# Loads and uses of turned tiles behind later weight tiles, two ways' outputs turned by TensorE, queries and keys ahead of the gated unit

## The chip, the cores and the metric

The kernel runs on one core of a Trainium2 chip. The metric is the time of one execution on the device in microseconds, as the median of several runs. The engines are TensorE (PE in the rows), VectorE (DVE), ScalarE (ACT), GpSimd (POOL) and SyncE (SP), which here issues all transfers.

## The reference

Two transformer blocks are computed one after the other for 256 tokens of width 1024, in fp32. The first block has two layers; each is a feed-forward, a mixer of three ways, and a feed-forward. The change touches the mixer of these two layers most:

```python
h = rms_norm(x, mix_norm[l])
uv, c_q, c_kv, k_rope, z, xbc, dt_raw, gates = jnp.split(h @ w_in[l], IN_OFFSETS, axis=-1)
y_a = gmlp_mixer(uv, ...)                # gated unit: gelu(u) * (W_s @ rms_norm(gelu(v)) + b)
y_b = mla_mixer(c_q, c_kv, k_rope, ...)  # causal attention, 8 heads, queries and keys from low ranks
y_c = ssd_mixer(z, xbc, dt_raw, ...)     # state-space way: convolution, scan over two chunks, gate z, norm
g = jax.nn.sigmoid(gates).reshape(bsz, s, N_BRANCH, D_MODEL)
merged = (g[:, :, 0] * (y_a @ w_branch[l, 0]) + g[:, :, 1] * (y_b @ w_branch[l, 1])
          + g[:, :, 2] * (y_c @ w_branch[l, 2]))
x = x + merged @ w_out[l]
```

A feed-forward is `(silu(h @ w_gate) * (h @ w_up)) @ w_down`. There are five of them, two in each layer and one in the second block, whose other parts (a mixer and a cross-attention) run the same helpers.

## The kernel before

**Weights.** All weights are read once from HBM, in tiles of 128 x 1024 fp32 (512 KB) or smaller. `wload` (line 158) issues a tile's transfer from SP into the ring `stage` (5 buffers), has ACT cast it to `whi` (line 165) and DVE subtract that from it into `wlo` (line 166); these two rings have 4 buffers each (`NW`). A product is three TensorE instructions (`mac`, lines 288 to 292): high part by high, high by low, low by high. So ACT can cast a weight tile only when TensorE is through with the tile four before it. `lin_tok` makes a product with tokens on the partitions for both token tiles of 128; eight k-blocks of 512 columns are four weight tiles, and a tile of two k-blocks feeds 12 instructions with 512 columns.

**Turning tiles.** What the next product contracts over has to stand on the partitions, so outputs are transposed. There are two ways. `to_T` (line 258) lets TensorE transpose blocks of 128 x 128 into a PSUM tile `tp`, from which ACT casts the high and DVE subtracts the low part (`split_evac`, lines 187 to 189). `flip` (line 267) lets DVE transpose blocks of 32 x 32 (line 273), writes the tile to a DRAM tile `flips` in four transfers (line 277), and reads it back in one, `flipped` (line 279), so that the blocks land in place; `flip_T` puts `split_evac` behind that. The rows of the next weight are stored in the order that this leaves (`ways`). Turned through DRAM are: the hidden tiles of the feed-forwards (hTh and hTl), the compressed queries and keys (cqT, ckvT), the queries and keys (qT, kT), and the outputs of the three ways: of the gated unit (yaT), of attention (ybT) and of the state-space way (ycT).

**The mixer.** `SEQ` lists its steps: x (the channels of the state-space way), u (the gated unit), q (queries, keys, values), z (its gate), S (the scan), A (attention), g0 to g2 (the gates of the three ways) and b0 to b2 (their output products, with yaT, ybT and ycT). The products of x, u, q, z, g and b stream weights. S and A have small products, exponentials and masks; they get a raised priority (`CPRIO`).

**What sets the order.** The code is written in the order of `SEQ`; a scheduler then sets each engine's stream from priorities and dependencies (weights have the highest priority, `WPRIO`). Each engine runs its stream in that order, and so does SP with its transfers. `issue_after` puts an instruction behind another in the order. The last b step in `SEQ` is b1, and the merged tile `mg` is then turned by `to_T` into mh and ml for the product with `m1_out`.

Of the kernel before, what the change touches and what calls it, by code (L numbers as in the profile page):

```python
# [8 lines left out]
F32 = mybir.dt.float32  # L9
# [7 lines left out]
P = 128  # L17
D = 1024
S = 256
# [12 lines left out]
BUFS = dict(  # L32
    sg=2, hb=1, flip=2, flipped=1,
    cg=2, xb=2, gv=2, gu=2, sq=2, q=2, k=2, kv=4, xs=2, xd=2, y=2, yo=2, jk=2, pr=2, pT0=2, pT1=2, ao=2, L=2, cbm=2, rp=2,
    D1=2, Mb=2, pm=2, XT=2, X=3, s5m0=2, s5x0=2, s5t=4, sq2=2, tg=1, o2=1, vn=2)
SEQ = "x u q z S A g0 b0 g2 g1 b2 b1"
NS, NW = 5, 4
COLS = ((0, 512), (512, 512))
LAST = ((0, 512), (512, 256), (768, 256))
# [27 lines left out]
class Net:  # L67
    def __init__(self, ctx, tc, a, outs):
        self.tc, self.nc, self.a, self.outs = tc, tc.nc, a, outs
        mk = lambda n, b=None, **k: ctx.enter_context(tc.tile_pool(name=n, bufs=b, **k))  # L70
        self.big = mk("big")
        self.sma, self.small = None, {}
        self.junk = mk("junk", 1)
        self.ps = mk("ps", space=PSUM)
        self.dram = mk("dram", 2, space=bass.MemoryType.DRAM)
        self.lane = ""
        self.wdma, self.ahead = [], []
        self.sma = Arena(self, 1536, "small")
        self.stage = self.A([NS, 1024], "stage")
        self.whi, self.wlo = [self.A([NW, 1024], n, F32R) for n in ("whi", "wlo")]  # L80
        nc = self.nc
        self.cst = Arena(self, 1024, "cst")
        self.triu = self.load(self.cst, a["c_triu"], [P, P], "triu")
        self.cmask = self.load(self.cst, a["c_cmask"], [P, P], "cmask")
        self.rowm = self.load(self.cst, a["c_rowm"], [P, 4], "rowm")
        self.ones = self.cst.tile([P, P])
        nc.vector.memset(self.ones, 1.0)
        self.mhalf = self.cst.tile([P, 8])
        nc.vector.memset(self.mhalf, -0.5)
        self.euler = self.cst.tile([P, 16])  # L90
        nc.vector.memset(self.euler, math.e)
        self.x = [self.A([D], f"x{t}") for t in range(2)]
# [58 lines left out]
    def _shape(t, shape):  # L151
# [4 lines left out]
        return t.rearrange("p (a b c) -> p a b c", b=shape[1], c=shape[2])  # L156

    def wload(self, src, shape):
        nc = self.nc
        n = int(np.prod(shape))  # L160
        i = len(self.wdma)
        with self.tc.high_priority(WPRIO):
            s, h, l = [ring[:, i % ring.shape[1], :n] for ring in (self.stage, self.whi, self.wlo)]
            self.wdma.append(self.dma(s, src, 4))
            nc.scalar.copy(h, s)  # L165
            self.wsub = nc.vector.tensor_tensor(l, s, h.bitcast(F32), ALU.subtract).ins  # L166
# [99 lines left out]

    def flip(self, src, w, rows=4):

# [4 lines left out]
        nc.vector.transpose(r, src)  # L273
        d = self.dram.tile([P, 512], F32, name="flips", tag="flips")[:32 * rows, :4 * w]
        to = d.rearrange("(j c) (i e) -> i c j e", c=32, e=w)
        for i in range(4):
            nc.sync.dma_start(out=to[i], in_=r[i * 32:i * 32 + 32].rearrange("p (j e) -> p j e", e=w))
        raw = self.A([512], "flipped")[:32 * rows, :4 * w]
        nc.sync.dma_start(out=raw, in_=d)
        return raw.rearrange("p (a k b) -> p a k b", a=4, b=32)  # L280

    def flip_T(self, src, n, hi, lo, t):

        tok = slice(t * P, (t + 1) * P)
        hi, lo = [z[:, :, tok].rearrange("p k (a b) -> p k a b", b=32) for z in (hi, lo)]
        self.split_evac(self.flip(src, n * 32).rearrange("p a k b -> p k a b"), hi, lo)

# [212 lines left out]
    def mixer1(self, l, norm, nxt):  # L500
# [38 lines left out]


        pas = self.lin_tok(xT, a["m1_cq"][l], 384)
        pbs = self.lin_tok(xT, a["m1_ckv"][l], 296)
# [58 lines left out]
        def heads():  # L601
# [3 lines left out]
            for hf in range(2):  # L605
# [4 lines left out]
                for t in range(2):  # L610
                    p, pk = pqs[t], pks[t]
                    with self.tc.high_priority(EPRIO):
# [27 lines left out]
                        for src, dst in ((q3, qT), (kk, kT)):  # L640
                            z = self.flip(src.rearrange("p b h c -> p (b h c)"), P, 3)
                            act.copy(dst[:96, :, toks[t]].rearrange("p h (a b) -> p h a b", b=32),
                                     z.rearrange("p a h b -> p h a b"))
                qkv.append((qT, kT, vv, sc))
# [15 lines left out]
        def ssd():  # L660
# [18 lines left out]
            for t in range(2):  # L679
# [59 lines left out]
                for g in range(2):  # L739
                    c = slice(g * S, (g + 1) * S)  # L740
                    stt(y[:, c], y[:, c], rg[:, g:g + 1], g_ssd[:, c], ALU.mult, ALU.mult)
                self.flip_T(y, 4, ycT[0], ycT[1], t)

        def attention():
            for hf in range(2):
                qT, kT, vv, sc = qkv[hf]
                for t in range(2):
# [30 lines left out]
                    for h in range(4):  # L778
                        for kb in range(t + 1):
                            pe.matmul(p[:, h * 64:(h + 1) * 64], pT[kb][:, h], vv[kb][:, h], start=kb == 0, stop=kb == t)  # L780
                    o = self.A([4, 64], "ao")
                    tt(o, self._shape(p[:, :256], [4, 64]), sm[:, :, None].to_broadcast([P, 4, 64]), ALU.mult)
                    self.flip_T(o.rearrange("p a b -> p (a b)"), 2, ybT[0][:, hf * 2:hf * 2 + 2],
                              ybT[1][:, hf * 2:hf * 2 + 2], t)
# [29 lines left out]
        for step in SEQ.split():  # L814
            i = int(step[1:] or 0)
            if step[0] == "b":
                branch(i, ys[i], not begun)
# [676 lines left out]
def _prep(inp):  # L1494
# [14 lines left out]
    cqw, ckvw, xbc, zz, uv, gg, uq, ukv, br = [], [], [], [], [], [], [], [], []  # L1509
    ways = (512,), (256, 256), (512,)  # L1510
    for l in range(2):
# [100 lines left out]
```

## Time and profile before

| | |
|---|---|
| median of 3 runs (lowest, highest) | 1687.34 us (1686.46, 1688.99) |
| the profiled execution, its span | 1684.87 us, 1683.2 us |
| TensorE busy, DVE, ACT, GpSimd | 98%, 68%, 54%, 5% of the span |
| mean granted clock of TensorE | 0.996 |
| chain that ended last: TensorE's share | 95% |

The durations below come from the profiled execution. TensorE's instructions are pipelined: the record of one is longer than the distance to the next, so the distance of starts tells what one costs. "Idle" is the time an engine stood still ahead of a group, and behind the arrow stands what ended most of it. PEclk is the clock that TensorE was granted, as a share of 2.4 GHz.

### The profile page before, as it was taken

The numbers are of one execution on the slowest core, as the hardware profiler recorded it, in microseconds if no ns is written. First come the engines' busy times: TensorE is split into PE (matmuls) and PEld (weight loads), VectorE is DVE, ScalarE is ACT, GpSimd is POOL, SyncE is SP. The second block draws the span as 40 slices with busy tenths as digits, with TensorE's granted clock in tenths as the row PEclk, the third lists the DMA queues.
The fourth block names the chain that finished last, engine by engine and source line by source line (L and its number), as shares of the span: only waits on it lengthen the run. The fifth ranks groups of instructions, "written<-read, shape, count | busy, mean of one in ns | idle before, by whom it ended". The sixth has DMA issues, their size and how long they took to land.

```text
span 1683.2 us, 24727 instructions
## 1 busy us (share of the span) xinstructions
PE 1653.3 (98%) x9090; PEld 1412.7 (84%) x9090; DVE 1152.4 (68%) x1904; ACT 904.5 (54%) x1361; POOL 80.7 (5%) x73
## 2 busy tenths in 40 slices
PE   8999999998999999999999989999999999999998
PEld 6888898887888888888988877888899888888888
DVE  5665599756666556665897666799689746756664
ACT  5444476663545444444676645545477555654443
POOL 0000013000000000000121000000010100000000
PEclk9999999999999999999999999999999999999999
DMA  7777577753687757776777645767764224347872
GB/s 258 242 239 246 178 225 235 225 179 122 193 252 249 230 176 237 248 242 184 230 232 232 191 147 188 225 211 235 230 196 144 64 63 154 123 151 246 260 234 98
DMA packets 158986, 337.15 MB, mean 200 GB/s; under 512 B 35984, under 2 KB 76432, under 8 KB 158864
## 3 DMA queue, kind: packets, MB, share of 16 engines
q1 hardware_dynamic: 158864, 335.57, 63.6%
q8 instruction: 71, 1.16, 0.3%
q14 instruction: 51, 0.42, 0.1%
HBM read 312.43 MB, written 23.07 MB: 199 GB/s over the span
## 4 chain that ended last, share of the span: by engine, by line
PE 95%; DVE 1%; ACT 1%; DMA 1%; issue 0%; SPq 0%; POOL 0%; POOLq 0%; DVEq 0%; ACTq 0%
PE mm L290 28%; PE mm L291 28%; PE mm L292 28%; PE tp L206 1%; PE mmm L290 1%; PE mmm L292 1%; PE mmm L291 1%; PE ch L758 1%; PE chs L1005 1%; PE ch L780 1%; PE ch L1143 0%; PE ch L721 0%; ACT whi L165 0%; PE tp L773 0%; PE ch L1138 0%
## 5 line engine op out<-in xcount | busy, mean ns | idle before, releaser
L166 DVE TENSOR_TENSOR wlo<-stage,whi 128x1024 fp32r<-128x1024 f32 (+3 forms) x552 | 659.6, 1199 | 331.6 <-ACT whi L165 313.1
L165 ACT CAST whi<-stage 128x1024 fp32r<-128x1024 f32 (+3 forms) x552 | 568.4, 1035 | 445.1 <-PE mm L292 366.0
L291 PE MATMUL mm<-wlo,xh 128*128 128x512 f32 (+3 forms) x1264 | 484.2, 385 | 0.0
L292 PE MATMUL mm<-whi,xl 128*128 128x512 f32 (+4 forms) x1264 | 481.0, 385 | 0.0
L290 PE MATMUL mm<-whi,xh 128*128 128x512 f32 (+3 forms) x1264 | 468.1, 385 | 0.1
L291 PEld LDWEIGHTS mm<-wlo,xh 128*128 128x128 f32 x1264 | 237.8, 188 | 45.7 <-DVE wlo L166 0.2
L290 PEld LDWEIGHTS mm<-whi,xh 128*128 128x128 f32 x1264 | 237.0, 188 | 45.9 <-ACT xh L210 0.5
L292 PEld LDWEIGHTS mm<-whi,xl 128*128 128x128 f32 x1264 | 236.8, 188 | 44.8
L292 PE MATMUL mm<-whi,hTl 128*128 128x512 f32 (+1 forms) x484 | 179.0, 370 | 0.0
L291 PE MATMUL mm<-wlo,hTh 128*128 128x512 f32 (+1 forms) x484 | 179.0, 370 | 0.0
L290 PE MATMUL mm<-whi,hTh 128*128 128x512 f32 (+1 forms) x484 | 178.8, 371 | 0.0
L174 POOL TENSOR_TENSOR small<-small,cst 128x1 f32<-128x1 f32 (+2 forms) x60 | 62.1, 1043 | 1154.1 <-DVE small L172 1110.1
L188 ACT CAST hTh<-flipped 128x512 fp32r<-128x512 f32 (+1 forms) x60 | 35.2, 587 | 132.5 <-DMA flipped<-flips 130.9
L292 PEld LDWEIGHTS mm<-whi,hTl 128*128 128x128 f32 x484 | 91.2, 188 | 15.5
L290 PEld LDWEIGHTS mm<-whi,hTh 128*128 128x128 f32 x484 | 91.2, 189 | 15.3
L291 PEld LDWEIGHTS mm<-wlo,hTh 128*128 128x128 f32 x484 | 91.3, 189 | 15.2
L189 DVE TENSOR_TENSOR hTl<-flipped,hTh 128x512 fp32r<-128x512 f32 (+1 forms) x60 | 38.8, 647 | 79.5 <-ACT hTh L188 75.3
L291 PE MATMUL mm<-xl,whi 128*128 128x256 f32 x320 | 90.7, 284 | 1.1 <-DVE xl L211 1.1
L290 PE MATMUL mm<-xh,whi 128*128 128x256 f32 x320 | 90.3, 284 | 1.2 <-ACT xh L210 1.2
L292 PE MATMUL mm<-xh,wlo 128*128 128x256 f32 x320 | 90.2, 283 | 0.0
L291 PEld LDWEIGHTS mm<-xl,whi 128*128 128x128 f32 x320 | 61.3, 192 | 1.6 <-DVE xl L211 1.5
L290 PEld LDWEIGHTS mm<-xh,whi 128*128 128x128 f32 x320 | 61.2, 192 | 1.4 <-ACT xh L210 1.4
(519 smaller groups left out, 2004.2 us busy)
## 6 DMA issues: line engine op xcount, KB each, us to landing
stage<-in_ffn_in SPq DMA_DIRECT2D x176, 512.0 KB, 4.3
stage<-in_ffn_out SPq DMA_DIRECT2D x88, 512.0 KB, 4.4
stage<-in_m_g SPq DMA_DIRECT2D x48, 512.0 KB, 4.6
stage<-in_f_in SPq DMA_DIRECT2D x44, 512.0 KB, 4.4
flips<-flip SPq DMA_DIRECT2D x232, 64.0 KB, 3.2
flipped<-flips SPq DMA_DIRECT2D x58, 256.0 KB, 3.6
stage<-in_m_br SPq DMA_DIRECT2D x24, 512.0 KB, 4.6
stage<-in_m_out SPq DMA_DIRECT2D x24, 512.0 KB, 3.6
```

The costliest lines, as they stand in the source:

```text
L165: nc.scalar.copy(h, s)
L166: self.wsub = nc.vector.tensor_tensor(l, s, h.bitcast(F32), ALU.subtract).ins
L174: nc.gpsimd.tensor_tensor(r, m, self.mhalf[:, :n], ALU.pow)
L188: self.nc.scalar.copy(hi, ps)
L189: self.nc.vector.tensor_tensor(lo, ps, hi.bitcast(F32), ALU.subtract)
L206: nc.tensor.transpose(p[:, k, t * P:(t + 1) * P], x[t][:, (k0 + k) * P:(k0 + k + 1) * P], self.ident)
L290: mm(out, lh, rh, start=first, stop=False)
L291: mm(out, lh, rl, start=False, stop=False)
L292: mm(out, ll, rh, start=False, stop=last)
L758: pe.matmul(p3[:, i], qT[:96, b * hb + i, toks[t]], kT[:96, b * hb + i, :nk], start=True, stop=True)
L780: pe.matmul(p[:, h * 64:(h + 1) * 64], pT[kb][:, h], vv[kb][:, h], start=kb == 0, stop=kb == t)
L1005: pe.matmul(q, self.s5bc[ct][:, 2 * (E5 - 1 - e) + i], um[:, :, e], start=e == 0, stop=e == E5 - 1)
```

## The change

`flip` gets the code that uses the turned tile as an argument (`use`) and issues only the turn and the four writes at once. The load is put down as due five weight tiles later and the use three tiles after that (`FLIPS`); `wload` issues what is due ahead of its tile, behind the last weight transfer and the last cast, and `flush` issues all that a step left open. `FLUSH` says where: the flips of the compressed queries and keys ahead of step q, those of q ahead of A, those of u ahead of b0. `flipped` has four buffers instead of one, and `flips` twelve instead of two. In `SEQ`, u moves from second place to behind x, z and q, and g0 comes between S and A. The outputs of the state-space way and of attention are turned by `to_T`; the weights of these ways are stored in natural row order accordingly (`ways`).

```diff
@@ -30,11 +30,13 @@
 ASIDE = 1
 BANKS = dict(mm=7, ch=3, tp=3, chs=4, tpm=2, mmm=3)
 BUFS = dict(
-    sg=2, hb=1, flip=2, flipped=1,
+    sg=2, hb=1, flip=2, flipped=4,
     cg=2, xb=2, gv=2, gu=2, sq=2, q=2, k=2, kv=4, xs=2, xd=2, y=2, yo=2, jk=2, pr=2, pT0=2, pT1=2, ao=2, L=2, cbm=2, rp=2,
     D1=2, Mb=2, pm=2, XT=2, X=3, s5m0=2, s5x0=2, s5t=4, sq2=2, tg=1, o2=1, vn=2)
-SEQ = "x u q z S A g0 b0 g2 g1 b2 b1"
+FLUSH = dict(q="k", A="q", b0="u")
+SEQ = "x z q u S g0 A b0 g2 g1 b2 b1"
 NS, NW = 5, 4
+FLIPS = 5, 3
 COLS = ((0, 512), (512, 512))
 LAST = ((0, 512), (512, 256), (768, 256))
 
@@ -74,7 +76,7 @@
         self.ps = mk("ps", space=PSUM)
         self.dram = mk("dram", 2, space=bass.MemoryType.DRAM)
         self.lane = ""
-        self.wdma, self.ahead = [], []
+        self.wdma, self.ahead, self.due, self.frees, self.step, self.seq = [], [], [], [0] * BUFS["flipped"], None, 0
         self.sma = Arena(self, 1536, "small")
         self.stage = self.A([NS, 1024], "stage")
         self.whi, self.wlo = [self.A([NW, 1024], n, F32R) for n in ("whi", "wlo")]
@@ -155,14 +157,33 @@
             return t.rearrange("p (a b) -> p a b", b=shape[1])
         return t.rearrange("p (a b c) -> p a b c", b=shape[1], c=shape[2])
 
+    def later(self, n, fn):
+
+        self.seq += 1
+        self.due.append((n, self.seq, self.step, fn))
+
+    def run_due(self, n):
+
+        while self.due and min(self.due)[0] <= n:
+            d = min(self.due)
+            self.due.remove(d)
+            with self.tc.issue_after(self.wdma[-1]), self.tc.issue_after(self.wcast):
+                d[3]()
+
+    def flush(self, step):
+
+        self.run_due(max([d[0] for d in self.due if d[2] == step], default=0))
+
     def wload(self, src, shape):
         nc = self.nc
+        if self.due:
+            self.run_due(len(self.wdma))
         n = int(np.prod(shape))
         i = len(self.wdma)
         with self.tc.high_priority(WPRIO):
             s, h, l = [ring[:, i % ring.shape[1], :n] for ring in (self.stage, self.whi, self.wlo)]
             self.wdma.append(self.dma(s, src, 4))
-            nc.scalar.copy(h, s)
+            self.wcast = nc.scalar.copy(h, s).ins
             self.wsub = nc.vector.tensor_tensor(l, s, h.bitcast(F32), ALU.subtract).ins
         return self._shape(h, shape), self._shape(l, shape)
 
@@ -264,26 +285,35 @@
         self.split_evac(self._shape(p[:, :n * P], [n, P]),
                         hi[:, :, t * P:(t + 1) * P], lo[:, :, t * P:(t + 1) * P])
 
-    def flip(self, src, w, rows=4):
+    def flip(self, src, w, use, rows=4):
+
 
 
         nc = self.nc
         n = rows * w
         r = self.A([512], "flip")[:, :n]
         nc.vector.transpose(r, src)
-        d = self.dram.tile([P, 512], F32, name="flips", tag="flips")[:32 * rows, :4 * w]
+        d = self.dram.tile([P, 512], F32, name="flips", tag="flips", bufs=12)[:32 * rows, :4 * w]
         to = d.rearrange("(j c) (i e) -> i c j e", c=32, e=w)
         for i in range(4):
             nc.sync.dma_start(out=to[i], in_=r[i * 32:i * 32 + 32].rearrange("p (j e) -> p j e", e=w))
-        raw = self.A([512], "flipped")[:32 * rows, :4 * w]
-        nc.sync.dma_start(out=raw, in_=d)
-        return raw.rearrange("p (a k b) -> p a k b", a=4, b=32)
+        at = max(len(self.wdma) + FLIPS[0], min(self.frees) + 1)
+        self.frees.remove(min(self.frees))
+        self.frees.append(at + FLIPS[1])
+        box = []
+
+        def load():
+            box.append(self.A([512], "flipped")[:32 * rows, :4 * w])
+            nc.sync.dma_start(out=box[0], in_=d)
+
+        self.later(at, load)
+        self.later(at + FLIPS[1], lambda: use(box[0].rearrange("p (a k b) -> p a k b", a=4, b=32)))
 
     def flip_T(self, src, n, hi, lo, t):
 
         tok = slice(t * P, (t + 1) * P)
         hi, lo = [z[:, :, tok].rearrange("p k (a b) -> p k a b", b=32) for z in (hi, lo)]
-        self.split_evac(self.flip(src, n * 32).rearrange("p a k b -> p k a b"), hi, lo)
+        self.flip(src, n * 32, lambda raw: self.split_evac(raw.rearrange("p a k b -> p k a b"), hi, lo))
 
     def mac(self, out, lh, ll, rh, rl, first, last):
         mm = self.nc.tensor.matmul
@@ -538,6 +568,7 @@
             rh.append(h)
 
 
+        self.step = "k"
         pas = self.lin_tok(xT, a["m1_cq"][l], 384)
         pbs = self.lin_tok(xT, a["m1_ckv"][l], 296)
         cqT = [self.A([3, S], "cqT", F32R) for _ in range(2)]
@@ -638,9 +669,9 @@
                         tt(kk[:, 2], kpe[t][:, None, :].to_broadcast([P, 4, 32]),
                            rk[:, :, None].to_broadcast([P, 4, 32]), ALU.mult)
                         for src, dst in ((q3, qT), (kk, kT)):
-                            z = self.flip(src.rearrange("p b h c -> p (b h c)"), P, 3)
-                            act.copy(dst[:96, :, toks[t]].rearrange("p h (a b) -> p h a b", b=32),
-                                     z.rearrange("p a h b -> p h a b"))
+                            to = dst[:96, :, toks[t]].rearrange("p h (a b) -> p h a b", b=32)
+                            self.flip(src.rearrange("p b h c -> p (b h c)"), P,
+                                      lambda z, to=to: act.copy(to, z.rearrange("p a h b -> p h a b")), 3)
                 qkv.append((qT, kT, vv, sc))
 
         def ssd_gate():
@@ -739,7 +770,7 @@
                 for g in range(2):
                     c = slice(g * S, (g + 1) * S)
                     stt(y[:, c], y[:, c], rg[:, g:g + 1], g_ssd[:, c], ALU.mult, ALU.mult)
-                self.flip_T(y, 4, ycT[0], ycT[1], t)
+                self.to_T(y, 4, ycT[0], ycT[1], t)
 
         def attention():
             for hf in range(2):
@@ -780,7 +811,7 @@
                             pe.matmul(p[:, h * 64:(h + 1) * 64], pT[kb][:, h], vv[kb][:, h], start=kb == 0, stop=kb == t)
                     o = self.A([4, 64], "ao")
                     tt(o, self._shape(p[:, :256], [4, 64]), sm[:, :, None].to_broadcast([P, 4, 64]), ALU.mult)
-                    self.flip_T(o.rearrange("p a b -> p (a b)"), 2, ybT[0][:, hf * 2:hf * 2 + 2],
+                    self.to_T(o.rearrange("p a b -> p (a b)"), 2, ybT[0][:, hf * 2:hf * 2 + 2],
                               ybT[1][:, hf * 2:hf * 2 + 2], t)
 
         mg = [self.A([D], "mg") for _ in range(2)]
@@ -813,6 +844,9 @@
         ys, begun = (yaT, ybT, ycT), False
         for step in SEQ.split():
             i = int(step[1:] or 0)
+            if step in FLUSH:
+                self.flush(FLUSH[step])
+            self.step = step
             if step[0] == "b":
                 branch(i, ys[i], not begun)
                 begun = True
@@ -1507,7 +1541,7 @@
     o["rope_freq"] = np.broadcast_to((1.0 / (10000.0 ** (np.arange(0, 32, 2) / 32.0))).astype(np.float32), (P, 16))
     w = inp["w_in"]
     cqw, ckvw, xbc, zz, uv, gg, uq, ukv, br = [], [], [], [], [], [], [], [], []
-    ways = (512,), (256, 256), (512,)
+    ways = (512,), (128,) * 4, (128,) * 4
     for l in range(2):
         wl = w[l]
         cqw.append(_blk(wl, 1024, 384, 2))
```

**b0 on ACT and TensorE.** In ACT's order before, in the first layer's mixer, the first cast of yaT stands among the query and key work; kv and sq are parts of that, whi is a weight tile:

```order
L615 ACTIVATE sq<-mm,small 128x384
L165 CAST whi<-stage 128x1024
L630 ACTIVATE sq<-kv 128x256
L165 CAST whi<-stage 128x1024
L188 CAST yaT<-flipped 128x4x128
L621 ACTIVATE kv<-mm,small 128x512
L615 ACTIVATE sq<-mm,small 128x384
L165 CAST whi<-stage 128x1024
L621 ACTIVATE kv<-mm,small 128x512
```

In the order now the casts of both token tiles stand here. The first whi is the last weight tile of b0, gt the last gate of g0, and what follows belongs to the scan:

```order
L674 COPY kT<-flipped 96x4x128
L186 CAST whi<-stage 128x1024
L827 ACTIVATE gt<-mm,small 128x512
L708 ACT_TABLE_LOAD
L708 ACTIVATE small<-small 128x8
L705 ACTIVATE small<-small 128x8
L716 COPY xs<-tp 128x512
L722 COPY bt<-tp 128x256
L209 CAST yaT<-flipped 128x4x128 x2
L729 COPY st<-ch 128x512
L746 ACTIVATE L<-ch,small 128x128 x8
```

The casts of yaT moved behind the last gate of g0 and the scan's first small steps, and behind a weight cast that waits for the last product of g0. On TensorE, before, at the first product with yaT (xh and xl are the normalized input, so those products belong to a gate):

```order
L292 MATMUL mm<-whi,xl 128x512
L689 MATMUL tp<-cst,xc 128x128 x2
L290 MATMUL mm<-whi,xh 128x512 x2
L290 MATMUL mm<-whi,yaT 128x512 x2
L291 MATMUL mm<-wlo,xh 128x512
L702 MATMUL tp<-xc 128x128 x2
L292 MATMUL mm<-whi,xl 128x512
L290 MATMUL mm<-whi,xh 128x512
```

and now, at the end of g0, with the scan's small products behind it:

```order
L320 MATMUL mm<-whi,xh 128x512
L321 MATMUL mm<-wlo,xh 128x512
L322 MATMUL mm<-whi,xl 128x512
L699 MATMUL tp<-small,cst 128x16
L702 MATMUL tp<-small,cst 128x8
L714 MATMUL tp<-cst,xc 128x128 x4
L720 MATMUL tp<-cst,xc 128x128 x2
L733 MATMUL tp<-xc 128x128 x2
L320 MATMUL mm<-whi,yaT 128x512
L321 MATMUL mm<-wlo,yaT 128x512
L727 MATMUL ch<-xdd,bt 128x256 x2
L506 MATMUL ch<-cst,small 128x128 x8
```

Products of a gate stood on both sides of the first use of yaT; now ten small products stand between the last product of g0 and that use.

**The turns of u on SP.** Before, the transfers of u's first token tile (4 x 128 columns; m_z and m_g are weight tiles):

```order
L100 DMA stage<-in_m_z 128x1024 x3
L277 DMA flips<-flip 32x4x128 x4
L100 DMA stage<-in_m_z 128x1024
L277 DMA flips<-flip 32x4x128
L279 DMA flipped<-flips 128x512
L277 DMA flips<-flip 32x4x128 x2
L100 DMA stage<-in_m_g 128x1024
L277 DMA flips<-flip 32x4x128
```

and now, with the turns of queries and keys (3 x 128 columns) ahead of them:

```order
L299 DMA flips<-flip 32x3x128
L307 DMA flipped<-flips 96x512
L299 DMA flips<-flip 32x3x128 x3
L299 DMA flips<-flip 32x4x128 x2
L307 DMA flipped<-flips 96x512
L299 DMA flips<-flip 32x4x128 x4
L307 DMA flipped<-flips 128x512
L299 DMA flips<-flip 32x4x128 x2
L102 DMA stage<-in_m_g 128x1024 x2
L307 DMA flipped<-flips 128x512
```

The writes and the load of u now stand between and behind loads of keys and queries, and the second load behind two weight tiles.

**The end of the mixer on TensorE.** Before, behind the last attention products (kv, pT) in the first layer:

```order
L780 MATMUL ch<-kv,pT_2803 128x64
L291 MATMUL mm<-wlo,ybT 128x512
L292 MATMUL mm<-whi,ybT 128x512
L263 MATMUL tp<-cst,mg 128x128 x4
L290 MATMUL mm<-whi,mh 128x512
L291 MATMUL mm<-wlo,mh 128x512
L263 MATMUL tp<-cst,mg 128x128 x4
L292 MATMUL mm<-whi,ml 128x512
L290 MATMUL mm<-whi,mh 128x512
L291 MATMUL mm<-wlo,mh 128x512
L292 MATMUL mm<-whi,ml 128x512
L290 MATMUL mm<-whi,ybT 128x512
```

and now from the same place on (ao is attention's output):

```order
L322 MATMUL mm<-whi,ybT 128x512 x2
L320 MATMUL mm<-whi,ybT 128x512
L321 MATMUL mm<-wlo,ybT 128x512
L322 MATMUL mm<-whi,ybT 128x512
L284 MATMUL tp<-cst,ao 128x128 x2
L320 MATMUL mm<-whi,ybT 128x512
L321 MATMUL mm<-wlo,ybT 128x512
L320 MATMUL mm<-whi,ybT 128x512
L321 MATMUL mm<-wlo,ybT 128x512
L284 MATMUL tp<-cst,mg 128x128 x4
L322 MATMUL mm<-whi,ybT 128x512
L320 MATMUL mm<-whi,ybT 128x512
```

Before, products with mh stood ahead of the last products with ybT, whose tile came from DRAM; now two transposes of ao stand there, and products with ybT of the other token tile around them.

## Rows read from the trace of the kernel before

**Rows 1.** the page's costliest groups: count, busy us, mean ns, idle before, releaser.
```profile
L188 ACT CAST hTh<-flipped 128x512 fp32r<-128x512 f32 (+1 forms) x60 | 35.2, 587 | 132.5 <-DMA flipped<-flips 130.9
...
L290 PE MATMUL mm<-whi,hTh 128*128 128x512 f32 (+1 forms) x484 | 178.8, 371 | 0.0
```

**Rows 2.** waits of PE: line, releaser, total us, times, longest us.
```profile
PE mm L290 <- ACT ybT L188: 7.5, 2, 4.4
...
PE mm L290 <- ACT mh L188: 2.7, 4, 0.7
```

**Rows 3.** windows: stretch, length, busy us (x) by engine, PEclk, DMA share, GB/s.
```profile
400.00:420.00 20.00, 16.28 (x63) 12.61 (x64) 9.49 (x13) 6.79 (x10) 0.00 (x0) 0.83 0.20 64
...
1000.00:1020.00 20.00, 14.06 (x55) 10.30 (x56) 9.31 (x15) 5.05 (x8) 0.00 (x0) 0.91 0.25 80
```

**Rows 4.** critical chain, end of the first layer's mixer: start, us, what.
```profile
380.11 1.78 PE ch L758 x8
...
389.40 0.87 PE tp L773 x8
...
398.26 0.36 DVE flip L273
...
403.62 0.41 ACT ybT L188
...
404.87 0.43 PE mm L291
...
409.13 0.44 PE mm L292
...
415.62 0.23 PE mm L292
```

**Rows 5.** the same chain at the second layer.
```profile
1000.24 0.36 DVE flip L273
...
1006.97 0.41 ACT ybT L188
```

**Rows 6.** timeline of ACT: start, us, engine line operation, idle before.
```profile
387.03 0.20 ACT L767 ACTIVATION_READ_ACCUMULATOR pr<-ch,small 128x1 f32 x1
```

**Rows 7.** groups of PE by form, 370 to 440 us: busy us, mean ns.
```profile
L773 PE MATMUL tp<-cst,pr 128*128 128x128 f32 x12 | 2.1, 272 | 0.0
```

**Rows 8.** timeline of ACT, the second of the two casts to yaT.
```profile
276.17 0.62 ACT L188 CAST yaT<-flipped 128x512 fp32r<-128x512 f32 x1 [1.55 <-DMA flipped<-flips]
```

**Rows 9.** timeline of PE, first use of yaT.
```profile
298.91 0.62 PE L290 MATMUL mm<-whi,yaT 128*128 128x512 f32 x2
```

**Rows 10.** ACT by form, 215 to 330 us: busy us, mean ns, idle.
```profile
L165 ACT CAST whi<-stage 128x1024 fp32r<-128x1024 f32 x37 | 38.7, 1048 | 9.2 <-PE mm L292 6.4 <-issue 2.5 <-PE mm L291 0.3
...
L796 ACT ACTIVATE gt<-mm,small 128x512 f32<-128x512 f32 x5 | 3.4, 682 | 1.0 <-PE mm L292 1.0
...
L642 ACT COPY kT<-flipped 96x512 f32<-96x512 f32 x4 | 2.5, 620 | 8.4 <-DMA flipped<-flips 8.4
...
L685 ACT COPY xs<-tp 128x512 f32<-128x512 f32 x2 | 1.2, 576 | 0.0
...
L691 ACT COPY bt<-tp 128x256 f32<-128x256 f32 x1 | 0.4, 366 | 0.0
```

**Rows 11.** timeline of ACT, a table load and the activation behind it.
```profile
297.53 1.28 ACT L677 ACT_TABLE_LOAD   x1
298.83 0.21 ACT L677 ACTIVATE small<-small 128x8 f32<-128x8 f32 x1
```

**Rows 12.** timeline of DVE, a query tile's turn.
```profile
270.80 0.57 DVE L273 STREAM_TRANSPOSE flip<-q 128x384 f32<-128x384 f32 x1
```

**Rows 13.** timeline of ACT, the same tile's copy.
```profile
283.07 0.62 ACT L642 COPY qT<-flipped 96x512 f32<-96x512 f32 x1 [0.77 <-DMA flipped<-flips]
```

**Rows 14.** DMA issues, 240 to 330 us: count, KB each, median us to landing.
```profile
flips<-flip SPq DMA_DIRECT2D x32, 48.0 KB, 3.7
flipped<-flips SPq DMA_DIRECT2D x8, 192.0 KB, 4.6
```

## The prediction

> **What bounds the kernel now.** I read the page's costliest groups first. Weight casts and flips cost ACT and DVE much, and the largest wait on a flip is that of the hidden tiles of the feed-forwards, 130.9 us; but the TensorE products that use them have no idle time in front of them [rows 1]. So that wait lies beside TensorE's work and is worth nothing. I then read TensorE's own waits: the flipped attention output ybT stopped it twice, for 7.5 us in all, and the merged output mh four times [rows 2]. Third, the windows: the two ybT waits lie at the end of the two mixers, where TensorE is busy 16.28 and 14.06 of 20 us and the granted clock falls to 0.83 and 0.91 [rows 3]. Last, the chain of waits there: turn on DVE, four writes, one load, cast, 5.0 us from the turn's end to the cast in the first layer and 6.4 in the second [rows 4, 5]. After that idle time products stand 0.43 us apart, against 0.23 later [rows 4]: TensorE runs at 1.2 instead of 2.4 GHz.
>
> **What the end of a mixer can give back.** Idle time in the two windows is 20 - 16.28 = 3.72 and 20 - 14.06 = 5.94 us. The missing clock is 0.17 x 20 = 3.4 and 0.09 x 20 = 1.8 us. That is 7.1 and 7.7, mean 7.4. A product's record ends some 0.17 us after the next could start (0.37 to 0.4 recorded [rows 1], 0.23 apart), so about five gaps hide 0.9 more: 8.3 us a layer. This goes, since both outputs are turned by TensorE and no DRAM trip is left there.
>
> Not all of it stays gone. The mh waits remain, four of 0.7 us in the kernel, 1.4 a layer [rows 2]. In the new order 19 products (19 x 0.23 = 4.4 us) stand between the last scores and the turns of the probabilities; in the trace of before the chain from the scores' end (380.11 + 1.78 = 381.89) to the last exponential's (387.23) takes 5.3 [rows 4, 6], so 0.9 is bare. The cast of ybT (0.41) is late by about 0.3 more. Together 2.6 back: net -5.7 us a layer, between -8.3 (nothing late) and -3.
>
> **The added turns.** Two token tiles of 4 blocks and four outputs of 2 are 16 TensorE transposes a layer. Eight take 0.87 us in the chain [rows 4], so 16 x 0.109 = 1.75 us, all on TensorE's path; bounds 1.6 and, at the recorded 0.272 each if nothing overlapped [rows 7], 4.4. I take 1.75, since the chain's row is spacing and the other is the record of a pipelined instruction. The DRAM transfers and DVE turns that go were beside other work, but for those counted above. The Trainium skill, in TensorE: Matmul & The Clock Gate, Part 4: PE-mode transpose, gives about 275 ns for one and says that such turns do not hold the clock up. The trace's 272 ns agrees as a duration, but not as a price: by the page's figure the sum would be 2.6 us a layer worse; of the clock, no row here has transposes alone for long enough.
>
> **The deferral.** In the feed-forwards the hidden tiles are now cast later, but by the order still three or more weight tiles (12 products, 2.8 us each) ahead of use: nothing, as cover exists before and after [rows 1]. If that cover failed, one trip's tail, up to 2 us, in each feed-forward. The turns of the compressed queries and keys are put off likewise, at nothing.
>
> **The new place of u.** This carries the forecast. Before, the second cast of yaT is at 276.17 and the first product that reads it at 298.91, 22 us later [rows 8, 9]. In the new order u comes after x, z and q, its turns after those of q and k on DVE and SP, and b0 directly behind g0. On ACT the cast of yaT stands behind the cast of b0's last weight tile. That cast waits for g0's last product, because it takes that tile's buffer. From that product on, ACT must do: weight cast 1.05, gate 0.68, table load 1.28, two small ones 0.42, xs 0.58, bt 0.37, yaT 0.62 [rows 8, 10, 11] = 5.0 us. TensorE has ten small products there, about 10 x 0.109 = 1.1 us; then comes the first product on yaT, and everything behind it. So TensorE waits at least 3.9 us in each layer. This is the lower bound and needs no transfer to be late.
>
> The transfers may add. A kT copy stands ahead of that weight cast on ACT, and it waits for the last k turn, which DVE reaches some 36 products (8.3 us) before g0's end. In this stretch of before one trip, from the end of q's turn (271.37) to its copy (283.07), took 11.7 us [rows 12, 13]; by medians a trip is 3.7 + 4.6 = 8.3 [rows 14]. The kT copy then ends 0.6 to 4.0 us after g0's last product, and the 5.0 us follow: TensorE waits 4.5 to 7.9. On SP the second half of u's writes waits behind that tile's load, which itself waits for its writes; if each takes the long trip, the load for u lands 10 us or more after g0 and the one of its second token tile, behind two weight loads, later still: 13 to 14 us is the upper bound. I take 6.5, towards the trip measured in this stretch. Behind idle time like this the clock fell in both mixers of before, at 3.4 and 1.8 us [rows 3]; I take the mean, 2.6, with 0 and 3.4 as ends. The Trainium skill, in ScalarE: Activation LUTs, What ACT_TABLE_LOAD costs, counts 2.66 us for a change of tables, the load and a drain. The trace has 1.28, with the next activation 0.02 us behind it [rows 11] and nothing idle ahead, so the row stands; by the page the wait would be 1.4 us longer.
>
> In z, q, u and g0 the steps change places, but by the order each weight tile's cast and subtraction have the same work ahead of them in sum, and TensorE waited for none of them there [rows 2]; I count nothing for that.
>
> **Sum.** Per layer -5.7 + 1.75 + 6.5 + 2.6 = +5.15; two layers +10.3. The profiled execution took 1684.87 us (span 1683.2 and 1.67 around it): 1695.2. The median of the runs shown is 2.47 above that execution, so about 1697 for a median run.
>
> **Rivals.**
> - *u arrives in time* (faster). If the cast of yaT lies beside products that the order does not seem to leave, the b0 term is 0: -5.7 + 1.75 = -3.95 a layer, 1687.3 - 7.9 = 1679.4. For it: in before the same cast was never waited for [rows 2]. Against it: the order on ACT, which no transfer speed mends. Its place is the first product on yaT; it decides for faster once wait plus lost clock stay under 3.95 us a layer. With the least wait of 3.9, no lost clock and less left at the end (1.7 instead of 2.6) it would be 1685, which is still no change.
> - *The short wait* (no change). ACT alone sets it, 3.9 us, and the clock holds: -5.7 + 1.75 + 3.9 = -0.05 a layer, 1687; with the smaller clock loss of 1.8, 1691.
> - *Trips in a row* (much slower). SP's queue decides: 13.5 us and 3.4 of clock, +12.95 a layer, 1713.
> - *The end of the mixer is only moved*: the tail keeps its idle time because softmax and merge are late instead. Bound above by 8.3 instead of 2.6 back: 11 us more, 1708. Against it: the only long step there now is the DRAM trip [rows 4, 5].
>
> **How the numbers follow.** The forecast (1691 to 1705) gets 0.55; faster by the first rival 0.2; the short wait 0.13; trips in a row or a moved tail 0.12. The range runs from the first rival's middle, 1680, to 1711 near the third's. 0.2%, 3.4 us, is about what a measurement can tell from no change: faster means under 1683.9, slower over 1690.7. The forecast and the last two give slower 0.66 (a part of the forecast's lower edge is lost to no change), the short wait and its neighbours 0.15, and faster 0.19.
>
> **What would show it.** In the profile after: no wait on ybT of over 1 us, and the windows at the mixers' ends near 19 of 20 us; a wait of TensorE on ACT's cast of yaT of 4 to 8 us, twice, ahead of it on ACT the table load and the weight cast, and products 0.43 us apart behind it; hTh still without idle time in front of its products. Wrong if the first yaT product follows its predecessors without a gap, if the clock stays at 2.4 GHz behind it, or if a wait of several us shows at a place that I gave nothing: the hidden tiles, or products on kT and qT.

## The result and the profile after

The changed kernel took 1700.57 us in the median of four runs (1700.41 to 1703.58), against 1687.46 for the kernel before (1686.46 to 1688.99): a ratio of 1.0081, 95% interval 1.0064 to 1.0099. It is slower by 13.1 us; 9.7 were forecast (1697 against 1687.3; the prediction's sum itself gives 10.3). The profiled execution took 1700.50 us with a span of 1698.8, 15.6 above before's; that is 2.5 more than between the medians, since before's profiled execution was 2.6 us faster than its median. The start times of the products show where these 15.6 went: from the last product with hTh of a layer's first feed-forward to the last with mh, and from the last with hTh of the second layer to the first of the second block.

| kernel | first layer's mixer | second layer's mixer | second block up to its hidden tiles |
|---|---|---|---|
| before | 240.0 us | 240.2 us | 392.7 us |
| changed | 245.2 us | 247.5 us | 396.2 us |

The mixers are 12.6 us longer, the second block 3.5, and other stretches 0.5 shorter in sum.

The waits of TensorE in the changed kernel (releaser, total us, times, longest us), where [rows 2] had 7.5 us on ybT and 2.7 on mh:

```profile
PE mm L320 <- ACT yaT L209: 16.3, 2, 9.0
...
PE mm L320 <- ACT ybT L209: 2.2, 4, 0.7
...
PE mm L320 <- ACT mh L209: 0.5, 2, 0.2
```

The wait has moved from ybT to yaT and is twice as long. The windows answer to [rows 3] (length, busy us of PE, PEld, DVE, ACT and POOL, clock, DMA share, GB/s):

```profile
300.00:320.00 20.00, 12.72 (x55) 10.20 (x54) 8.66 (x15) 12.53 (x26) 0.00 (x0) 0.74 0.60 189
400.00:420.00 20.00, 18.64 (x101) 15.00 (x100) 13.60 (x20) 9.39 (x22) 0.00 (x0) 1.00 0.34 105
900.00:920.00 20.00, 10.99 (x52) 8.78 (x51) 11.36 (x21) 11.59 (x18) 0.00 (x0) 0.84 0.69 200
920.00:940.00 20.00, 20.00 (x98) 17.04 (x97) 10.72 (x16) 12.78 (x31) 0.70 (x1) 0.90 0.48 168
1000.00:1020.00 20.00, 18.88 (x101) 15.75 (x100) 14.14 (x23) 8.61 (x19) 0.00 (x0) 1.00 0.49 156
```

At the ends of the mixers (400 to 420 and 1000 to 1020 us) TensorE is now busy 18.64 and 18.88 of 20 us, at full clock. The hole is at 300 to 320 and 900 to 920, with 12.72 and 10.99 busy. The timeline of TensorE in the first layer (start, us, line, operation, idle before and releaser) shows it: last product of g0, the last of the ten small products, then the first with yaT.

```profile
299.19 0.39 PE L322 MATMUL mm<-whi,xl 128*128 128x512 f32 x1
...
300.47 0.61 PE L733 MATMUL tp<-xc 128*128 128x128 f32 x4
308.36 0.80 PE L320 MATMUL mm<-whi,yaT 128*128 128x512 f32 x1 [7.28 <-ACT yaT L209]
308.95 0.63 PE L321 MATMUL mm<-wlo,yaT 128*128 128x512 f32 x1
```

ACT's timeline in the same stretch:

```profile
300.08 0.62 ACT L674 COPY qT<-flipped 96x512 f32<-96x512 f32 x1 [2.19 <-DMA flipped<-flips]
...
303.27 0.62 ACT L674 COPY kT<-flipped 96x512 f32<-96x512 f32 x1 [1.04 <-DMA flipped<-flips]
303.80 1.04 ACT L186 CAST whi<-stage 128x1024 fp32r<-128x1024 f32 x1
304.74 0.68 ACT L827 ACTIVATE gt<-mm,small 128x512 f32<-128x512 f32 x1
305.44 1.28 ACT L708 ACT_TABLE_LOAD   x1
...
306.95 0.57 ACT L716 COPY xs<-tp 128x512 f32<-128x512 f32 x1
307.42 0.38 ACT L722 COPY bt<-tp 128x256 f32<-128x256 f32 x1
307.68 0.63 ACT L209 CAST yaT<-flipped 128x512 fp32r<-128x512 f32 x1
```

This is the chain that the prediction counted: behind the copy of kT come the weight cast, the gate, the table load, xs, bt and the cast of yaT, without a gap, 303.80 to 308.31. Its start is late, since the copy of kT waited for its load until 303.27, while g0's last product started at 299.19. The issues of SP show why (start, time with the queue, count):

```profile
296.84 2.37 SPq L299 DMA_DIRECT2D flips<-flip  x5
300.71 0.32 SPq L307 DMA_DIRECT2D flipped<-flips  x1
301.07 1.88 SPq L299 DMA_DIRECT2D flips<-flip  x4
303.99 0.34 SPq L307 DMA_DIRECT2D flipped<-flips  x1
...
307.25 0.33 SPq L307 DMA_DIRECT2D flipped<-flips  x1
```

Of the first five writes, three are the key tile's and two are of u's first token tile; they stand behind the load of a query tile (296.48) in SP's order. The load of the key tile is issued at 300.71. Only behind it go the other two writes of u's first tile, with two of the second's, and at 303.99 the load of u's first tile. It lands some 2.7 us later, at about 306.7, when ACT was still busy with other things until 307.68. So ACT's chain ended last here, by one us. In the second layer the wait is 9.01 us by the same chain. The products behind it run at half rate for a while; the chain of waits in the second layer has (start, us, what)

```profile
918.93 0.43 PE mm L321
...
923.48 0.43 PE mm L320
...
924.26 0.24 PE mm L322
```

so the clock there is back from 1.2 to 2.4 GHz at 924.26: a product takes 0.43 us until then and 0.24 from there on. The deferral did what was said of the hidden tiles: ACT's wait on their loads fell from 130.9 us [rows 1] to 63.2, and TensorE's products still have no idle time in front:

```profile
L320 PE MATMUL mm<-whi,hTh 128*128 128x512 f32 (+1 forms) x484 | 178.9, 371 | 0.0
...
L209 ACT CAST hTh<-flipped 128x512 fp32r<-128x512 f32 (+1 forms) x60 | 34.6, 581 | 64.7 <-DMA flipped<-flips 63.2
```

### The profile page after: what moved, and what is told of

Read it like the earlier page. It is cut to its first block, busy times and chain, and to the rows that moved or that the text cites. A ratio compares the mean times of both kernels' runs of the same rounds, so it can differ in the third digit from the quotient of the medians.

```text
span 1698.8 us, 24768 instructions
## 1 busy us (share of the span) xinstructions
PE 1658.9 (98%) x9122; PEld 1417.5 (83%) x9122; DVE 1146.3 (67%) x1892; ACT 909.1 (54%) x1361; POOL 76.2 (4%) x73
## 4 chain that ended last, share of the span: by engine, by line
PE 90%; DVE 3%; DMA 3%; ACT 2%; issue 1%; SPq 1%; POOL 0%; POOLq 0%; DVEq 0%; ACTq 0%
PE mm L320 27%; PE mm L321 26%; PE mm L322 26%; DMA flips<-flip 1%; DVE wlo L187 1%; PE tp L227 1%; PE mmm L320 1%; PE mmm L322 1%; PE mmm L321 1%; PE ch L789 1%; ACT whi L186 1%; PE chs L1039 1%; PE ch L811 1%; DMA stage<-in_m_g 1%; PE ch L1177 0%
## 5 line engine op out<-in xcount | busy, mean ns | idle before, releaser
L320 PEld LDWEIGHTS mm<-whi,xh 128*128 128x128 f32 x1264 | 236.9, 188 | 45.5 <-ACT xh L231 0.5
L322 PEld LDWEIGHTS mm<-whi,xl 128*128 128x128 f32 x1264 | 236.9, 188 | 45.0
L209 ACT CAST hTh<-flipped 128x512 fp32r<-128x512 f32 (+1 forms) x60 | 34.6, 581 | 64.7 <-DMA flipped<-flips 63.2
```

The lines of the kernel that those rows point to most:

```text
L209: self.nc.scalar.copy(hi, ps)
L320: mm(out, lh, rh, start=first, stop=False)
L322: mm(out, ll, rh, start=False, stop=last)
```

## The experiments

Two theories stand against each other at first. Theory 1: the new place of u makes TensorE wait at b0, and costs more than the ends of the mixers give. Rival: the deferral or the added turns cost the time. Four kernels ran side by side; the kernel before took 1686.75 us there (23 runs).

**The changed kernel in the old order.**

```diff
-SEQ = "x z q u S g0 A b0 g2 g1 b2 b1"
+SEQ = "x u q z S A g0 b0 g2 g1 b2 b1"
-    flipped=4
+    flipped=2
```

> The changed kernel with the old order of steps (u second, g0 behind A), with two buffers of flipped instead of four, since four do not fit with that order; deferral and TensorE turns stay. Theory 1 (the new place of u costs what the ends of the mixers give): the wait on yaT, 16.3 us in all in the changed kernel, goes to under 1 us, with the lost clock behind it; the mixers end as in the changed kernel. What is left is the 3.4 us that the second block takes longer, if that comes with the deferral: 1680 to 1684. Rival (deferral or the turns on TensorE cost it): it stays within 4 us of the changed kernel's 1700.6.

Measured: 1682.75 us (12 runs, 1679.47 to 1688.32), ratio to before 0.9982 (0.997 to 0.9994). The windows that had the hole:

```profile
300.00:320.00 20.00, 20.00 (x106) 17.10 (x105) 10.71 (x15) 12.86 (x25) 0.00 (x0) 1.00 0.73 251
900.00:920.00 20.00, 17.29 (x90) 14.38 (x89) 10.05 (x13) 12.21 (x24) 0.00 (x0) 0.99 0.70 231
```

The wait on yaT is gone, and with it 17.8 us of the changed kernel's time (by the medians). Theory 1 holds; the rival falls. In the second layer 2.71 us of idle time show, in two waits for the scan's masks on DVE; the mixers take 235.5 and 240.3 us. The kernel is still 3.4 us behind the next one, which has the turns without the deferral.

**The turns by TensorE alone.**

```diff
-                self.flip_T(y, 4, ycT[0], ycT[1], t)
+                self.to_T(y, 4, ycT[0], ycT[1], t)
-                    self.flip_T(o.rearrange("p a b -> p (a b)"), 2, ...
+                    self.to_T(o.rearrange("p a b -> p (a b)"), 2, ...
-    ways = (512,), (256, 256), (512,)
+    ways = (512,), (128,) * 4, (128,) * 4
```

> The kernel before with one edit: the outputs of attention and of the state-space way turned by TensorE, with the weight rows in natural order. Theory 1: wait on ybT and lost clock at the mixers' ends go, 16 turns a layer are added, the second block has before's order: 1687.4 - 2 x 4 = 1679.5, and with the end measured in the changed kernel (6.9 a layer less) nearer 1677. Rival (the end only moves its wait from the DRAM trip to softmax and merge, so the turns' 3.5 us come on top): 1687 to 1691.

Measured: 1679.39 us (1678.06 to 1681.76), ratio 0.9962 (0.9948 to 0.9976), as forecast from before's rows. Its waits at the end of the mixers, and two windows there and two of the second block:

```profile
PE tp L263 <- DVE ao L782: 1.0, 2, 0.5
PE mm L290 <- ACT ybT L188: 0.9, 2, 0.5
```

```profile
380.00:400.00 20.00, 18.82 (x104) 15.41 (x103) 13.87 (x26) 9.00 (x20) 0.00 (x0) 1.00 0.40 132
400.00:420.00 20.00, 19.70 (x94) 16.06 (x93) 13.92 (x18) 10.67 (x15) 0.00 (x0) 1.00 0.40 131
...
1420.00:1440.00 20.00, 17.76 (x130) 17.03 (x129) 13.27 (x24) 11.03 (x18) 1.08 (x2) 0.91 0.36 112
1440.00:1460.00 20.00, 18.18 (x141) 17.95 (x140) 13.35 (x26) 12.50 (x24) 0.00 (x0) 0.91 0.47 155
```

About 1.5 us of idle time is left at a mixer's end, and the rival falls. The mixers take 235.5 and 236.9 us, 4.4 and 3.2 less than before's. The last two rows are of the second block and are taken up below.

**The deferral alone.**

```diff
-FLUSH = dict(q="k", A="q", b0="u")
+FLUSH = dict(q="k", A="q", b0="u", b2="S", b1="A")
-SEQ = "x z q u S g0 A b0 g2 g1 b2 b1"
+SEQ = "x u q z S A g0 b0 g2 g1 b2 b1"
```

and `flip_T` and `ways` for the two outputs as in the kernel before.

> The changed kernel with the old order of steps and with attention's and the state-space way's outputs turned through DRAM again, flushed ahead of b1 and b2: the deferral alone. Theory 1: it is worth nothing where TensorE works (hidden tiles had no wait), and brings the second block's 3.4 us: 1690 to 1692, with waits on ybT at least as long as before's 7.5 us. If the second block's 3.4 us come from the order of steps instead: 1687. Rival (the deferral frees SP and ACT and is a gain by itself): under 1684.

Measured: 1688.94 us (12 runs, 1685.90 to 1691.89), ratio 1.0016 (1.0006 to 1.0025): between the two values that were expected, slower by 1 to 4 us. The waits at the mixers' ends are nearly those of before (on ybT 6.6 us, where at least 7.5 were expected), so the deferral by itself is no gain:

```profile
PE mm L320 <- ACT ybT L209: 6.6, 2, 4.3
...
PE mm L320 <- ACT mh L209: 3.0, 4, 0.9
...
PE mm L320 <- ACT st L729: 1.7, 2, 1.5
...
PE mm L321 <- DVE wlo L187: 1.5, 2, 0.8
```

The last two waits are new; they stand near the first products with yaT (315 to 321 us and 917 to 922). The mixers take 240.6 and 243.7 us.

**The new order alone.**

```diff
-SEQ = "x u q z S A g0 b0 g2 g1 b2 b1"
+SEQ = "x z q u S g0 A b0 g2 g1 b2 b1"
```

> The kernel before with one edit: the new order of steps. Loads and uses follow the turns at once, all outputs go through DRAM. Theory 1: TensorE waits for yaT at b0 in both layers with several us and runs at 1.2 GHz behind it, while the ends of the mixers stay as they were: 1703 to 1714. Rival (u comes late only through the deferral, which puts its load and cast behind later weights): no wait on yaT of over 2 us, 1686 to 1690.

Measured: 1700.87 us (1695.64 to 1702.09; the profiled execution took 1696.15), ratio 1.0082 (1.0064 to 1.0099): the order alone costs as much as the whole change, and the rival, that u is late only through the deferral, falls. Two things were not as expected. First, the wait at b0 is mostly not in front of yaT. The timeline of TensorE:

```profile
301.06 0.61 PE L702 MATMUL tp<-xc 128*128 128x128 f32 x4
306.73 2.04 PE L696 MATMUL ch<-xdd,bt 128*128 128x256 f32 x4 [5.06 <-DVE xdd L693]
308.56 1.91 PE L476 MATMUL ch<-cst,small 128*128 128x128 f32 x8
312.74 0.79 PE L290 MATMUL mm<-whi,yaT 128*128 128x512 f32 x1 [2.26 <-ACT L L715]
```

Here the scan's state product stands ahead of yaT and waits 5.06 us for xdd, which DVE makes from xs; ACT copies xs behind a weight cast, a gate and the table load. Second, the ends of the mixers did not stay as they were:

```profile
400.00:420.00 20.00, 18.09 (x87) 14.74 (x86) 15.65 (x22) 7.41 (x9) 0.00 (x0) 1.00 0.52 172
1000.00:1020.00 20.00, 18.82 (x88) 15.43 (x87) 18.29 (x25) 8.17 (x9) 0.00 (x0) 1.00 0.61 199
```

TensorE is busy 18.09 and 18.82 us there, with no wait on ybT, though ybT still came through DRAM. Behind the last attention products 44 and 48 products with ycT, some 10 us, now stand ahead of those with ybT, where before had none. So in the new order attention is early enough without the turns by TensorE, which leaves these little to give; that is why the time is below the expected range.

The next four kernels ran beside the kernel before at 1686.26 us (23 runs); the first two ask what u is late by.

**The changed kernel with u turned by TensorE.** (`flipped=2`.)

```diff
-                self.flip_T(u, 4, yaT[0], yaT[1], t)
+                self.to_T(u, 4, yaT[0], yaT[1], t)
-    ways = (512,), (128,) * 4, (128,) * 4
+    ways = (128,) * 4, (128,) * 4, (128,) * 4
```

> The changed kernel, new order of steps, with the gated unit's output turned by TensorE too (two buffers of flipped). No DRAM trip is left for u, and the cast of yaT stands ahead of b0's last weight casts on ACT. Theory 1 (the wait at b0 is the trip together with the cast's place on ACT): no wait on yaT, nothing at 1.2 GHz there; 8 turns more a layer add 1.75 us in all: 1681 to 1687. Rival (ACT's other work, casts behind copies of keys, holds TensorE up at b0 whatever u does): still over 4 us of waiting a layer, 1693 or more.

Measured: 1681.54 us (1678.59 to 1682.51), ratio 0.997 (0.9958 to 0.9982). The rival falls; no wait on yaT is left, and the window of the hole is full:

```profile
300.00:320.00 20.00, 20.00 (x98) 16.48 (x97) 14.49 (x20) 16.41 (x29) 0.00 (x0) 1.00 0.71 242
```

**One more gate ahead of b0.**

```diff
-SEQ = "x z q u S g0 A b0 g2 g1 b2 b1"
+SEQ = "x z q u S g0 A g2 b0 g1 b2 b1"
```

> The changed kernel with one more gate ahead of b0 (g2 between A and b0): 96 products, 22 us, stand between g0's end and the first use of yaT. Theory 1 (u is late by 8 to 9 us and TensorE has nothing else): wait and lost clock at b0 go, 1680 to 1686. Rival (loads are flushed ahead of b0, so the wait moves with b0): still over 3 us on yaT in each layer, 1692 or more. The second block has the changed kernel's order here; if that order costs its 3.5 us, they show between the last mh and the last feed-forward.

Measured: 1683.05 us (1680.79 to 1685.97), ratio 0.9984 (0.9975 to 0.9992).

```profile
300.00:320.00 20.00, 20.00 (x108) 17.07 (x107) 11.64 (x17) 15.06 (x29) 0.00 (x0) 1.00 0.75 246
320.00:340.00 20.00, 20.00 (x99) 16.76 (x98) 16.48 (x24) 13.48 (x26) 0.70 (x1) 1.00 0.58 183
```

No wait on yaT is left, and the rival falls: TensorE lacked work behind g0, and 96 products of another gate are enough. u is still turned through DRAM and behind the keys here, and the whole hole is gone.

**Copies of queries and keys on DVE.**

```diff
-   lambda z, to=to: act.copy(to, ...)
+   lambda z, to=to: v.tensor_copy(to, ...)
```

> The changed kernel with the copies of turned queries and keys made by DVE instead of ACT, so that ACT's weight casts no longer stand behind a copy that waits for a load. Theory 1 (two chains end within about 1 us of each other, ACT's, and on SP the load of u behind the trips of the keys): the wait at b0 falls by at most 1.5 us a layer, 1697 to 1701. Rival (the copy of kT that holds ACT is the cause): it falls by the 3.2 to 4.6 us that ACT's last weight cast stood behind it, and part of the lost clock: 1690 or less.

Measured: 1698.71 us (1695.68 to 1699.46), ratio 1.0071 (1.0058 to 1.0084). ACT's casts are free of the copies, but TensorE now waits for DVE, whose small operation L696 (302.94 us) stands behind the copy of kT:

```profile
PE tp L699 <- DVE small L696: 8.3, 2, 5.0
...
PE ch L727 <- DVE xdd L724: 4.5, 2, 2.2
```

```profile
302.60 0.42 DVE L674 COPY kT<-flipped 96x512 f32<-96x512 f32 x1 [0.95 <-DMA flipped<-flips]
```

That is 12.8 us instead of 16.3. The time hardly moved, as theory 1 expected, but not for its reason, and the rival's cause is not refuted: the same copy holds DVE's queue here instead of ACT's. Whether the load of u was a second chain cannot be told, as the wait went to DVE's queue before that could show.

**All three outputs turned by TensorE, old order.** The edit of the turns-only kernel and, for u, that of the kernel with u turned by TensorE.

> The kernel before, old order of steps, no deferral, with all three outputs turned by TensorE: the turns-only kernel (1679.4) plus u. Theory 1: the cast of yaT was never waited for there, so nothing is won and 16 turns in two layers cost 16 x 0.109 = 1.75 us: 1681. Rival (less traffic on SP and the queues helps other trips): 1678 or less.

Measured: 1682.03 us (12 runs, 1681.26 to 1689.25), ratio 0.9987 (0.9976 to 0.9999); the turns-only kernel had 0.9962. In the two mixers TensorE is busy for 470.4 us in all, against 468.7 in the turns-only kernel, at full clock in both, and idle for 3.6 against 3.8: turning what was not waited for costs 1.8 us and wins next to nothing. The medians do not show this price by itself, since the second block has another order of products here and is 1.7 us longer than the turns-only kernel's (below).

**Attention's output alone, old order.** If a turn by TensorE pays only where TensorE waited for the DRAM trip, ycT should stay with DRAM too. Beside it the turns-only kernel ran again, before at 1684.27 us (15 runs).

```diff
-                    self.flip_T(o.rearrange("p a b -> p (a b)"), 2, ...
+                    self.to_T(o.rearrange("p a b -> p (a b)"), 2, ...
-    ways = (512,), (256, 256), (512,)
+    ways = (512,), (128,) * 4, (512,)
```

> The kernel before with attention's output alone turned by TensorE; the state-space way's and the gated unit's stay with DRAM. Theory 1 (a turn by TensorE pays only where TensorE waited for the DRAM trip; it waited for ybT and not for ycT): the same gain at the mixers' ends as the turns-only kernel has, and 8 turns a layer less, 1.75 us in all: 1677 to 1679. Rival (the state-space way's trips fill SP's queue ahead of attention's and cost too): no better than the turns-only kernel, 1680 or more.

> The turns-only kernel once more, beside the kernel with attention's output alone on the same chip, so that 1.75 us between them can be told: 1679 to 1680.

Measured: 1673.37 us (1670.73 to 1674.64), ratio 0.9935 (0.9922 to 0.9947), and 1680.07, ratio 0.9972 (0.9961 to 0.9983). The best version, 0.65% faster than before, and better than expected: beside the 1.75 us of turns, the idle time at the mixers' ends is nearly gone:

```profile
380.00:400.00 20.00, 19.97 (x104) 16.62 (x103) 14.97 (x25) 10.07 (x20) 0.00 (x0) 1.00 0.38 131
400.00:420.00 20.00, 19.68 (x95) 16.10 (x94) 14.81 (x19) 10.30 (x14) 0.00 (x0) 1.00 0.50 153
```

Between the last scores and the first turn of their probabilities 32 products with ycT and ybT stand in this kernel's order and 12 in the turns-only kernel's, so the softmax is covered. A mixer takes 233.1 and 233.3 us, where the turns-only kernel took 235.5 and 238.0 in the run beside it.

## Why the prediction was right, step by step

**The wait at b0: right in mechanism, too small in size.** Place, releaser and the queue on ACT were as forecast. The lower bound of 3.9 us from ACT alone and the upper one of 13 to 14 held the measured 7.28 and 9.01; 6.5 was taken, and the mean is 8.15. The second wait lies above the 4 to 8 us that were to show. What was mis-sized is how early DVE turns the last key tile: it was to reach that turn 8.3 us before the end of g0's last product (299.42 and 907.46), and the turn ended 5.7 and 4.3 us before it.

```profile
293.11 0.57 DVE L295 STREAM_TRANSPOSE flip<-k 128x384 f32<-128x384 f32 x1
...
902.60 0.57 DVE L295 STREAM_TRANSPOSE flip<-k 128x384 f32<-128x384 f32 x1
```

Shortly ahead of it, before a weight subtraction, DVE had stood idle for 2.2 and 3.5 us, waiting for a weight cast of ACT. The trip from the turn's end to the copy took 9.6 and 9.9 us, within the 8.3 to 11.7 of the prediction. So the copy of kT, which was to end 0.6 to 4.0 us after g0's last product, ended 4.5 us (303.89) and in the second layer 6.2 us after it. ACT's chain behind the copy took 4.5 us, where 5.0 were added up from records that overlap a little.

**The clock behind it: right, in part by luck.** TensorE ran at half rate from 308.36 to 313.23 and from 918.13 to 924.26 us (a product with 512 columns took 0.43 us there), 4.9 and 6.1 us, which costs 2.4 and 3.1; 2.6 was taken. The clock column shows more, 5.2 us missing in either layer ((1 - 0.74) x 20, and (0.16 + 0.10) x 20), since the clock fell already during the wait, where it costs nothing. The 2.6 came from that column; read in the same way, these two waits would have been priced at 5.2, above the prediction's upper end of 3.4.

**The end of the mixers: right as a sum, but the cause was named too narrowly.** Of 8.3 us a layer 5.7 net were to come back. From the mixers' length, 6.3 longer in the mean, less 1.75 of turns, 8.15 of wait and 2.75 of clock, 6.35 came back; this is what is left over, so it holds the deferral's cost too. In the turns-only kernel the mixers are 4.4 and 3.2 us shorter, where 3.95 were counted for the ends and the turns together. But the prediction said that this comes from the turns by TensorE. The order alone removes the wait on ybT as well, at the price of the hole at b0. The turns alone in the old order bring it down to 0.9 us too. In the changed kernel both were paid for and only one was needed.

**The turns: right.** With u's 16 turns added in the old order, TensorE is busy in the mixers for 470.4 us, against 468.7 and 468.8 in the two profiles of the turns-only kernel: 1.6 to 1.8 us, where 16 x 0.109 = 1.75 is the spacing's price. The Trainium skill (TensorE: Matmul & The Clock Gate, Part 4: PE-mode transpose) gives about 275 ns for a turn; as a price for each of the 16 that would be an estimate of 4.4 us, which these runs do not bear out.

**The deferral and the second block: the step that was mis-sized.** Both were given nothing. The hidden tiles were indeed free. But the deferral alone measures 1 to 4 us slower, and with the turns in the old order it is 3.4 us slower than the turns alone. In the profiles this time lies in the mixers: 240.6 and 243.7 us with the deferral alone against before's 240.0 and 240.2, and a second mixer of 240.3 against 236.9 with the turns. Which of the deferred loads and casts makes it was not tried apart.

The second block is 3.5 us longer in the changed kernel, at full clock in all windows of both. Its TensorE order differs from before's there, although the edit touches only its feed-forward, and TensorE is idle for 7.6 us against 6.2. No edit of the change brings this order by itself: taken instruction by instruction, the turns alone and the order alone have before's, and so have the deferral alone and the deferral with the turns, but for six of some 2850. The kernel with a gate between has the changed kernel's, and so has, but for six, the one with all three outputs turned, which has neither deferral nor new order. What makes the scheduler choose it stays open. Its price can be read from two profiles in which about as much clock is missing in this block, some 3.5 us each: it takes 398.8 us in the kernel with a gate between and 395.6 in the turns-only kernel. With the 3.5 us between the changed kernel and before, both at full clock, 3.2 to 3.5 us belong to that order.

The rivals fell: u was not in time, the wait was not the short one, trips did not stand in a row for 13 us, and the mixer's end kept only 1.4 and 1.1 us of idle time in the two windows. Between the two profiles the sum reads 10.3 forecast, 3.3 more of wait at b0, 0.3 more of clock, 1.3 more back at the mixers' ends, 3.5 in the second block and 0.5 less elsewhere: 15.6.

## What to carry to other kernels

A step that is moved to right before its consumer is priced by what else the consumer's engine has to do there: read from the new order how many products stand between, and from the old trace what the engines in front must still finish behind the last of them. An instruction that waits for a load holds everything behind it on its engine, and moving it to another engine can move the wait: 16.3 us for ACT became 12.8 for DVE. Take a faster but costlier route only for the one transfer that the bounding engine waits for: turning attention's output alone was worth 0.65%, attention's and the state-space way's 0.28 to 0.38%, and the whole change cost 0.81%. Compare the order of instructions also in parts that the edit does not touch: here a scheduler's other choice in the second block cost 3.2 to 3.5 us.

## What the runs showed of the hardware

The granted clock in the second block differs between executions of the same order of products. In before's profiled execution every window there is at 1.00; in the turns-only kernel's the windows at 1420 to 1460 us have 0.91, above, and some 3.5 us are missing in sum over that block. The idle time of TensorE is the same in both, 6.2 and 6.1 us, with the longest waits (1.2, 1.1 and 1.8 us) in front of the same products. The block takes 392.7 us in the one and 395.6 in the other, so the missing clock cost just under 3 us. The runs of the kernel before spread from 1681.15 us, with a mean clock of 0.997, to 1688.71, with 0.994, so differences of 3 us in single profiles say little without the clock column.
